# Strassen's algorithm for the down projection of ten channel groups, laid between the blocks of the up projection

## The chip, the cores and the metric

The kernel runs on one core of one Trainium2 chip. The metric is the device time of one execution in microseconds; a profiled execution gives the trace, whose span goes from the first to the last instruction. The core has five engines that matter here: TensorE (PE in the trace, PEld for its weight loads), VectorE (DVE), ScalarE (ACT), GpSimd (POOL) and SyncE (SP), which issues the transfers.

## What is computed

One layer of a bidirectional encoder, 512 tokens by 2048 channels, all in float32: a norm, one input projection, windowed attention beside chunked spatial gating, an output projection, and then the gated MLP, which is where the change is.

```python
def conv_ffn(h, w_up, conv_w, conv_b, w_down):
    a = h @ w_up                              # (512, 2048) x (2048, 11264)
    a = depthwise_conv(a, conv_w) + conv_b    # width 3 over the positions
    g, u = a[..., :D_FF], a[..., D_FF:]       # D_FF = 5632
    return (silu(g) * u) @ w_down             # (512, 5632) x (5632, 2048)
...
x = x + conv_ffn(rmsnorm(x, norm2_g), w_up, conv_w, conv_b, w_down)
return rmsnorm(x, final_g)
```

## The kernel before

Every large product is made of three matmuls in the type float32r. Each operand is split into a high part (a cast on ACT) and a low part (the operand minus its high part, on DVE), and `mm3` (L77 to L80) adds high x high, high x low and low x high in one PSUM bank. Weights come in units of 128 x 1024 floats (512 KB): `weights` (L65 to L75) loads a unit on SP's queue (L72), casts it on ACT (L73) and subtracts on DVE (L74). The pool `wp` has three buffers each for the unit as loaded, its high part and its low part.

The MLP has 44 tiles of 128 channels, in 11 groups of four (`NGRP`, `GF`). `up(i)` (L432 to L457) makes tile i: four units with 24 matmuls of 512 tokens each, for two PSUM banks (gate and linear part). In the last unit the first bank gets its 12 matmuls before the second. Then the tile is drained: for each bank the product with the norm (`a`, L445, DVE), the middle tap of the convolution (`c`, L448, ACT) and the two outer taps (L450 and L451, DVE), and then the SiLU (L454, ACT), the product (`sg`, L455, DVE), and the split of the result into `ah` and `al` (L456 ACT, L457 DVE).

`down(g, act)` (L466) takes a group of four tiles as 512 channels of the inner dimension: for each of four blocks of 512 output columns two units of `w_down`, and for each of four token tiles one PSUM bank with 4 x 3 matmuls (`down_part`, L459), added to the residual stream `x2[t][c]` on DVE (L464). The loop over the groups writes the four `up` blocks of group g and behind them `down(g - 1)`. The last group's down projection (from L486) runs token tile by token tile with the final norm behind each; its weights are split in `split` (L82).

PSUM has eight banks: four in the pool `psm` (the up blocks take two at a time) and four in `pss` (the down projection and all small products). SBUF has 64 slots of 128 x 512 floats in `big` (`slot`): sixteen hold `x2`, 32 the split input `hs` of the MLP. The pool `oct` has four tiles of 8 KB a partition, in the MLP for `ah` and `al`. The order in which an engine gets its instructions is drawn up when the program is built; it follows the text, but an instruction that is ready can go ahead of one that is not.

Of the kernel before, what the change touches and what calls it, by code (L numbers as in the profile page):

```python
# [47 lines left out]
def hymba_block(ctx, tc, xT, x, w_in, w_up, w_out, w_down, wsT, cols, brow, frow, srow, rel, out):  # L48
    nc = tc.nc
    const = ctx.enter_context(tc.tile_pool(name="const", bufs=1))  # L50
    big = ctx.enter_context(tc.tile_pool(name="big", bufs=NSLOT))
    wp = ctx.enter_context(tc.tile_pool(name="wp", bufs=3))
    oct = ctx.enter_context(tc.tile_pool(name="oct", bufs=4))
    tmp = ctx.enter_context(tc.tile_pool(name="tmp", bufs=2))
    small = ctx.enter_context(tc.tile_pool(name="small", bufs=4))
    psm = ctx.enter_context(tc.tile_pool(name="psm", bufs=4, space=bass.MemoryType.PSUM))
    pss = ctx.enter_context(tc.tile_pool(name="pss", bufs=4, space=bass.MemoryType.PSUM))

    def f(ap):
        return ap.bitcast(F32)  # L60
# [3 lines left out]

    def weights(src, name, parts=1):  # L65
        st = wp.tile([P, 1024], F32, tag="wst", name=f"st_{name}")
        hi = wp.tile([P, 1024], F32R, tag="whi", name=f"hi_{name}")
        lo = wp.tile([P, 1024], F32R, tag="wlo", name=f"lo_{name}")
        n = 1024 // parts
        for i in range(parts):  # L70
            cs = slice(i * n, (i + 1) * n)
            nc.sync.dma_start(st[:, cs], src[:, cs])  # L72
            nc.scalar.copy(hi[:, cs], st[:, cs])  # L73
            nc.vector.tensor_tensor(lo[:, cs], st[:, cs], f(hi[:, cs]), op=ALU.subtract)  # L74
        return hi, lo  # L75

    def mm3(ps, a, b, start, stop):  # L77
        nc.tensor.matmul(ps, a[0], b[0], start=start, stop=False)  # L78
        nc.tensor.matmul(ps, a[0], b[1], start=False, stop=False)  # L79
        nc.tensor.matmul(ps, a[1], b[0], start=False, stop=stop)  # L80

# [11 lines left out]
    def rsqrt_v(v, n, name, pool=None):  # L93
        """1 / sqrt(v) over [P, n], by Newton's iteration; -RS_K / sqrt(v) if n is 1."""
        pool = pool or small
        r = pool.tile([P, n], F32, tag=f"{name}_r" if pool is const else f"rs_r{n}", name=f"{name}_r")
        t = small.tile([P, n], F32, tag=f"rs_t{n}", name=f"{name}_t")
        nc.vector.tensor_single_scalar(t.bitcast(I32), v.bitcast(I32), 1, op=ALU.logical_shift_right)
        nc.vector.tensor_scalar(r.bitcast(I32), t.bitcast(I32), -1.0, float(0x5F3759DF), op0=ALU.mult, op1=ALU.add)
        for i in range(3):  # L100
            if n == 1:
                nc.vector.scalar_tensor_tensor(t, r, v, r, op0=ALU.mult, op1=ALU.mult)
                nc.vector.scalar_tensor_tensor(r, t, RS_C[i], r, op0=ALU.add, op1=ALU.mult)
            else:
# [12 lines left out]
    col = const.tile([P, N_COLS], F32, name="col")  # L117
# [119 lines left out]
    for t in range(NT):  # L237
# [192 lines left out]

    # ---- gated MLP with the convolution over positions
    def up(i, ah, al):  # L432
        pst = [psm.tile([P, S], F32, tag="m", name=f"up{i}_{j}") for j in range(2)]
        for u in range(4):
            hi, lo = weights(w_up[4 * i + u], f"u{i}_{u}")
            hv = hi.rearrange("p (k j c) -> p k j c", k=4, c=P)
# [6 lines left out]
        for j in range(2):  # L443
# [8 lines left out]
            cv.append(t)  # L452
        sg = slot(F32, f"sg{i}")
        nc.scalar.activation(sg, cv[0], AF.Silu)  # L454
        nc.vector.tensor_tensor(sg, sg, cv[1], op=ALU.mult)  # L455
        nc.scalar.copy(ah, sg)  # L456
        nc.vector.tensor_tensor(al, sg, f(ah), op=ALU.subtract)  # L457

    def down_part(g, act, c, t, un, cs=slice(0, S)):  # L459
        ps = pss.tile([P, S], F32, tag="s", name=f"dn{g}{c}{t}")[:, cs]  # L460
        for k in range(GF):
            a = tuple(z[:, k, t * P : (t + 1) * P] for z in act)
            mm3(ps, a, tuple(z[:, cs] for z in un[k]), k == 0, k == GF - 1)
        nc.vector.tensor_tensor(x2[t][c][:, cs], x2[t][c][:, cs], ps, op=ALU.add)  # L464

    def down(g, act):  # L466
        for c in range(4):
            un = []
            for u in range(2):
                hi, lo = weights(w_down[(g * 4 + c) * 2 + u], f"d{g}{c}{u}")  # L470
                un += [(hi[:, :S], lo[:, :S]), (hi[:, S:], lo[:, S:])]
            for t in range(NT):
                down_part(g, act, c, t, un)

    acts = {}
    for g in range(NGRP):
        ah = oct.tile([P, GF, S], F32R, tag="oct", name=f"ah{g}")
        al = oct.tile([P, GF, S], F32R, tag="oct", name=f"al{g}")
        for k in range(GF):
            up(GF * g + k, ah[:, k, :], al[:, k, :])  # L480
        acts[g] = (ah, al)
        if g >= 1:
            down(g - 1, acts.pop(g - 1))

    # ---- the last group of channels, token tile by token tile, and the final norm
    g = NGRP - 1  # L486
    fg = [slot(F32, f"fg{c}") for c in range(4)]
    un = []
    for c in range(4):
        un.append([])  # L490
        for u in range(2):
            st = wp.tile([P, 1024], F32, tag="wst", name=f"st_l{c}{u}")
            nc.sync.dma_start(st, w_down[(g * 4 + c) * 2 + u])
            for k in range(2):
                un[c].append(split(st[:, k * S : (k + 1) * S], f"dl{c}{u}{k}"))
        nc.sync.dma_start(fg[c], frow[c * S : (c + 1) * S].partition_broadcast(P))
        nc.vector.tensor_scalar_mul(fg[c], fg[c], -1.0 / RS_K)
    for t in range(NT):
        ssf = small.tile([P, 5], F32, tag="ssf", name=f"ssf{t}")
        pre = small.tile([P, 1], F32, tag="pre", name=f"pre{t}")  # L500
        for c in range(4):
            xt = x2[t][c]
            if c < 3:
                down_part(g, acts[g], c, t, un[c])
                junk = slot(F32, f"jf_{c}{t}")
                nc.scalar.activation(junk, xt, AF.Square, accum_out=ssf[:, c : c + 1])
                nc.vector.tensor_tensor(xt, xt, fg[c], op=ALU.mult)
            else:
                junk = slot(F32, f"jf_{c}{t}")
                for i in range(2):  # L510
                    cs = slice(i * 256, i * 256 + 256)
                    down_part(g, acts[g], c, t, un[c], cs)
                    nc.scalar.activation(junk[:, cs], xt[:, cs], AF.Square, accum_out=ssf[:, c + i : c + i + 1])
# [17 lines left out]
def _units(w, ncols):  # L531
    """[K, n] -> [units, 128, 1024]: for each ncols columns, 1024 / ncols row tiles a unit."""
    K, n = w.shape
# [9 lines left out]
def _layout(x, norm1_g, w_in, gmlp_v_norm_g, gmlp_ws, gmlp_b, attn_sink, attn_out_norm_g,  # L543
# [10 lines left out]
    w3 = np.concatenate([_units(wo[:1024], 512), _units(wo[1024:], 512)])  # L554
    w4 = np.concatenate([_units(wd[g * GF * P : (g + 1) * GF * P], 512) for g in range(NGRP)])
    cw, cb = np.asarray(conv_w)[0], np.asarray(conv_b)[0]
# [34 lines left out]
```

## Time and profile before

| | us |
|---|---|
| median of 3 runs | 2002.8 |
| lowest and highest run | 1999.89 and 4076.22 |
| span of the profiled execution | 1999.4 |
| PE busy in that span | 1986.3 |
| DVE busy | 993.2 |
| ACT busy | 623.0 |
| matmuls (records) | 9016 |

The table's busy times are sums over the whole span. PE's matmuls are pipelined: a row's duration is longer than the time to the next row. A view by windows tells how busy each engine was in a stretch and at what share of its full speed TensorE's clock was granted; a timeline gives each instruction's start and duration, and in brackets how long its engine had been idle and who released it.

### The profile page before, as it was taken

What the parts mean: (1) busy time and instruction counts of PE and PEld (TensorE: products, weight loads), DVE (VectorE), ACT (ScalarE), POOL (GpSimd) and SP (SyncE); (2) the same over time, 40 slices, a digit from 0 to 9 for tenths busy, and PEclk for the clock granted to TensorE, in tenths of its full rate; (3) what the DMA queues carried; (4) which work ended last, traced back from release to release, by engine and by line L of the source; (5) the groups of instructions that cost most, each with busy time, mean ns of one, the idle gap of its engine ahead of it and who ended that gap; (6) DMA issues with size and microseconds to landing.
All of it is one profiled execution on the core that took longest, in us unless ns stands there. A gap on an engine that the chain in (4) does not pass through costs nothing.

```text
span 1999.4 us, 21966 instructions
## 1 busy us (share of the span) xinstructions
PE 1986.3 (99%) x9016; PEld 1648.8 (82%) x9016; DVE 993.2 (50%) x1350; ACT 623.0 (31%) x825; POOL 56.2 (3%) x60
## 2 busy tenths in 40 slices
PE   9999999999999999999999999999999999999998
PEld 7988888888888888888888888888888888888887
DVE  7376573434454454444445444444445454454466
ACT  6243442312333332323323223232232232322333
POOL 5001101000000000000000000000000000000000
PEclk9999999999999999999999999999999999999999
DMA  6222232532223323233232232222332223322242
GB/s 219 86 73 74 74 106 94 170 100 88 95 85 100 101 84 106 96 95 102 88 106 95 95 102 99 95 95 95 98 102 95 95 95 98 103 94 96 95 148 84
DMA packets 59572, 201.06 MB, mean 101 GB/s; under 512 B 6864, under 2 KB 7120, under 8 KB 59472
## 3 DMA queue, kind: packets, MB, share of 16 engines
q1 hardware_dynamic: 59472, 199.67, 30.5%
q8 instruction: 70, 1.15, 0.2%
q14 instruction: 30, 0.25, 0.0%
HBM read 195.44 MB, written 4.19 MB: 100 GB/s over the span
## 4 chain that ended last, share of the span: by engine, by line
PE 97%; issue 1%; DVE 1%; POOL 0%; ACT 0%; DMA 0%; SPq 0%; ACTq 0%; DVEq 0%; POOLq 0%
PE up L80 16%; PE up L78 16%; PE up L79 16%; PE dn L79 8%; PE dn L78 8%; PE dn L80 8%; PE pj L78 3%; PE pj L79 3%; PE pj L80 3%; PE u L78 1%; PE u L79 1%; PE u L80 1%; PE vg_ps L78 1%; PE vg_ps L79 1%; PE vg_ps L80 1%; PE g L79 1%
## 5 line engine op out<-in xcount | busy, mean ns | idle before, releaser
L80 PE MATMUL up<-h_h,lo_u 128*128 128x512 f32 x1408 | 547.9, 389 | 0.0
L78 PE MATMUL up<-h_h,hi_u 128*128 128x512 f32 x1408 | 547.9, 389 | 0.0
L79 PE MATMUL up<-h_l,hi_u 128*128 128x512 f32 x1408 | 547.8, 389 | 0.0
L74 DVE TENSOR_TENSOR lo_u<-st_u,hi_u 128x1024 fp32r<-128x1024 f32 x176 | 215.3, 1224 | 362.8 <-ACT hi_u L73 362.8
L73 ACT CAST hi_u<-st_u 128x1024 fp32r<-128x1024 f32 x176 | 185.6, 1055 | 471.5 <-PE up L79 377.8
L79 PEld LDWEIGHTS up<-h_l,hi_u 128*128 128x128 f32 x1408 | 264.4, 188 | 54.8
L80 PEld LDWEIGHTS up<-h_h,lo_u 128*128 128x128 f32 x1408 | 264.4, 188 | 54.8
L78 PEld LDWEIGHTS up<-h_h,hi_u 128*128 128x128 f32 x1408 | 264.4, 188 | 54.6
L78 PE MATMUL dn<-hi_d,ah 128*128 128x512 f32 x640 | 249.0, 389 | 0.0
L79 PE MATMUL dn<-lo_d,ah 128*128 128x512 f32 x640 | 249.0, 389 | 0.0
L80 PE MATMUL dn<-hi_d,al 128*128 128x512 f32 x640 | 249.0, 389 | 0.0
L464 DVE TENSOR_TENSOR x<-x,dn 128x512 f32<-128x512 f32 (+1 forms) x180 | 121.2, 674 | 138.2 <-PE dn L80 137.2
L73 ACT CAST hi_d<-st_d 128x1024 fp32r<-128x1024 f32 x80 | 84.4, 1055 | 306.3 <-PE dn L80 208.2
L74 DVE TENSOR_TENSOR lo_d<-st_d,hi_d 128x1024 fp32r<-128x1024 f32 x80 | 97.8, 1223 | 137.1 <-ACT hi_d L73 137.1
L78 PEld LDWEIGHTS dn<-hi_d,ah 128*128 128x128 f32 x640 | 120.2, 188 | 25.0
L79 PEld LDWEIGHTS dn<-lo_d,ah 128*128 128x128 f32 x640 | 120.2, 188 | 24.9
L80 PEld LDWEIGHTS dn<-hi_d,al 128*128 128x128 f32 x640 | 120.2, 188 | 24.9
L74 DVE TENSOR_TENSOR lo_i<-st_i,hi_i 128x1024 fp32r<-128x1024 f32 (+1 forms) x57 | 72.8, 1277 | 75.6 <-ACT hi_i L73 75.4
L448 ACT ACTIVATE c<-a,col 128x512 f32<-128x512 f32 x88 | 71.8, 816 | 120.8 <-DVE a L445 120.8
L73 ACT CAST hi_i<-st_i 128x1024 fp32r<-128x1024 f32 (+1 forms) x57 | 58.8, 1033 | 121.9 <-PE u L79 38.7
L74 DVE TENSOR_TENSOR lo_o<-st_o,hi_o 128x1024 fp32r<-128x1024 f32 x32 | 39.2, 1225 | 95.5 <-ACT hi_o L73 95.5
L450 DVE SCALAR_TENSOR_TENSOR c<-a,col,c 128x511 f32<-128x511 f32 x88 | 65.8, 748 | 38.9 <-ACT c L448 38.9
(243 smaller groups left out, 2264.3 us busy)
## 6 DMA issues: line engine op xcount, KB each, us to landing
st_u<-in_w_up SPq DMA_DIRECT2D x176, 512.0 KB, 3.3
st_d<-in_w_down SPq DMA_DIRECT2D x80, 512.0 KB, 3.3
st_i<-in_w_in SPq DMA_DIRECT2D x55, 512.0 KB, 3.3
st_o<-in_w_out SPq DMA_DIRECT2D x32, 512.0 KB, 3.3
xg<-in_xT SPq DMA_DIRECT2D x16, 256.0 KB, 4.8
x<-in_x SPq DMA_DIRECT2D x16, 256.0 KB, 5.7
st_l<-in_w_down SPq DMA_DIRECT2D x8, 512.0 KB, 3.5
out<-x SPq DMA_DIRECT2D x16, 256.0 KB, 2.9
```

The lines of the kernel that those rows point to most:

```text
L73: nc.scalar.copy(hi[:, cs], st[:, cs])
L74: nc.vector.tensor_tensor(lo[:, cs], st[:, cs], f(hi[:, cs]), op=ALU.subtract)
L78: nc.tensor.matmul(ps, a[0], b[0], start=start, stop=False)
L79: nc.tensor.matmul(ps, a[0], b[1], start=False, stop=False)
L80: nc.tensor.matmul(ps, a[1], b[0], start=False, stop=stop)
L448: nc.scalar.activation(t, a, AF.Identity, scale=w[1], bias=col[:, C_CB + j * 44 + i : C_CB + j * 44 + i + 1])
L450: nc.vector.scalar_tensor_tensor(t[:, 1:], a[:, : S - 1], w[0], t[:, 1:], op0=ALU.mult, op1=ALU.add)
L464: nc.vector.tensor_tensor(x2[t][c][:, cs], x2[t][c][:, cs], ps, op=ALU.add)
```

## The change

The groups 0 to 9 no longer use `down`. Their 512 tokens, 512 channels and 2048 columns are cut into halves (tokens: 256 and 256; channels: the even and the odd of the four tiles; columns: for each m in 0 and 1 the blocks m and 2 + m), and for each m the eight products of quarters are replaced by seven after Strassen, in the form with shared sums. `act_forms` makes the seven left factors (three plain quarters' splits beside four sums' splits: 11, 12, 22, s1, s2, s3, s4) once a group, from a float32 tile `act`. `down` makes the right factors from four loaded quarters (three plain ones, t1, t2, t3, t4), some in place, splits them with `halves`, and adds the products to the residual tiles and to `accu`, which collects what three of the four output quarters share over all groups. A product is twelve matmuls of 512 columns on two banks; two of the seven go on in banks that were read before.

A group's part is written as four functions, `first` and `second` for m = 0 and m = 1, and each is called behind one of the next group's four `up` blocks: `first` (four products: 11, s3, 12, 22) behind the first and third, `second` (s1, s2, s4) behind the second and fourth. `up` no longer splits its result. After the loop `accu` is added to the residual tiles and the last group's activations are split; its down projection is as before.

The pools `wp` and `oct` are closed ahead of the MLP. New pools stand in their place: `wq` with three buffers each for high and low parts, `raw` with six for loaded units and for t3, `acp` with one for `act`, `afp` with seven for the left factors. The layout of `w_down` in memory is changed to fit the quarters; a load is still 512 KB.

```diff
+    front.close()
+    wp = ctx.enter_context(tc.tile_pool(name="wq", bufs=3))
+    raw = ctx.enter_context(tc.tile_pool(name="raw", bufs=6))
+    acp = ctx.enter_context(tc.tile_pool(name="acp", bufs=1))
+    afp = ctx.enter_context(tc.tile_pool(name="afp", bufs=7))
...
-        sg = slot(F32, f"sg{i}")
-        nc.scalar.activation(sg, cv[0], AF.Silu)
-        nc.vector.tensor_tensor(sg, sg, cv[1], op=ALU.mult)
-        nc.scalar.copy(ah, sg)
-        nc.vector.tensor_tensor(al, sg, f(ah), op=ALU.subtract)
+        nc.scalar.activation(cv[0], cv[0], AF.Silu)
+        nc.vector.tensor_tensor(dst, cv[0], cv[1], op=ALU.mult)
...
+    def act_forms(g, act):
+        q = {(th, kh): act[:, kh::2, th * 256 : (th + 1) * 256] for th in range(2) for kh in range(2)}
...
+        put("11", q[0, 0])
+        put("s3", sum2(q[0, 0], q[1, 0], ALU.subtract, "s3"))
+        put("12", q[0, 1])
+        put("22", q[1, 1])
+        s1 = sum2(q[1, 0], q[1, 1], ALU.add, "s1")
+        put("s1", s1)
+        s2 = sum2(s1, q[0, 0], ALU.subtract, "s2")
+        put("s2", s2)
+        put("s4", sum2(q[0, 1], s2, ALU.subtract, "s4"))
+        return out
...
+        def product(a, st, name, pst, start):
+            hi, lo = halves(st, f"{name}{n}")
+            for t in range(2):
+                for k in range(2):
+                    w = tuple(z[:, k * S : (k + 1) * S] for z in (hi, lo))
+                    mm3(pst[t], tuple(z[:, k, t * P : (t + 1) * P] for z in af[a]), w, start and k == 0, k == 1, True)
...
+        def into(dst, pst):
+            for d, ps in zip(dst, pst):
+                nc.vector.tensor_tensor(d, d, ps, op=ALU.add)
...
+        def first():
+            b["11"] = q(0, 0)
+            b["12"], b["22"] = q(0, 1), q(1, 1)
+            pa = bank("dp1")
+            product("11", b["11"], "b11", pa, True)
+            into(accu[m], pa)
+            t3 = raw.tile([P, 1024], F32, tag="raw", name=f"t3_{n}")
+            sub(t3, b["22"], b["12"])
+            pb = bank("dp7")
+            product("s3", t3, "t3", pb, True)
+            into(c22, pb)
+            b["21"] = q(1, 0)
+            product("12", b["21"], "b21", pa, False)
+            into(c11, pa)
+            b["t1"] = sub(b["12"], b["12"], b["11"])
+            b["t2"] = sub(b["11"], b["22"], b["t1"])
+            t4 = sub(b["21"], b["21"], b["t2"])
+            product("22", t4, "t4", pb, False)
+            into(c21, pb)
+
+        def second():
+            pa = bank("dp5")
+            product("s1", b["t1"], "t1", pa, True)
+            into(c22, pa)
+            pb = bank("dp6")
+            product("s2", b["t2"], "t2", pb, True)
+            into(accu[m], pb)
+            product("s4", b["22"], "b22", pa, False)
+            into(c12, pa)
...
     for g in range(NGRP):
+        act = acp.tile([P, GF, S], F32, tag="act", name=f"act{g}")
+        parts = [p for m in range(2) for p in down(g - 1, m, af)] if g else [None] * GF
         for k in range(GF):
-            up(GF * g + k, ah[:, k, :], al[:, k, :])
-        acts[g] = (ah, al)
-        if g >= 1:
-            down(g - 1, acts.pop(g - 1))
+            up(GF * g + k, act[:, k, :])
+            if parts[k]:
+                parts[k]()
+        if g < NGRP - 1:
+            af = act_forms(g, act)
+    for m in range(2):
+        for t in range(2):
+            for d in (x2[t][2 + m], x2[2 + t][m], x2[2 + t][2 + m]):
+                nc.vector.tensor_tensor(d, d, accu[m][t], op=ALU.add)
```

## Rows read from the trace of the kernel before

**Rows 1.** The page: the span, and each engine's busy us, share, instructions.
```profile
span 1999.4 us, 21966 instructions
...
PE 1986.3 (99%) x9016; PEld 1648.8 (82%) x9016; DVE 993.2 (50%) x1350; ACT 623.0 (31%) x825; POOL 56.2 (3%) x60
```

**Rows 2.** Waits of PE: who for whom, total, times, longest.
```profile
PE r_ps L144 <- POOL xsq L166: 2.0, 1, 2.0
```

**Rows 3.** Windows: stretch, length, busy PE, PEld, DVE, ACT, POOL, clock, DMA, GB/s.
```profile
50.00:200.00 150.00, 149.87 (x792) 126.61 (x791) 84.00 (x155) 51.77 (x102) 10.00 (x20) 1.00 0.24 78
...
1180.00:1304.00 124.00, 124.00 (x549) 102.71 (x548) 60.14 (x71) 34.36 (x39) 0.00 (x0) 1.00 0.30 98
...
1990.00:1999.40 9.40, 0.26 (x3) 0.06 (x1) 3.46 (x14) 1.84 (x4) 0.00 (x0) 0.69 0.32 112
```

**Rows 4.** Timeline around the end of an up block: start, duration, engine, instruction.
```profile
1245.23 1.23 DVE L74 TENSOR_TENSOR lo_d<-st_d,hi_d 128x1024 fp32r<-128x1024 f32 x1 [4.26 <-ACT hi_d L73]
...
1249.57 0.39 PE L78 MATMUL dn<-hi_d,ah 128*128 128x512 f32 x1
...
1250.08 0.68 DVE L445 TENSOR_TENSOR a<-up,r_b 128x512 f32<-128x512 f32 x1
...
1250.68 1.22 DVE L74 TENSOR_TENSOR lo_d<-st_d,hi_d 128x1024 fp32r<-128x1024 f32 x1
...
1251.82 0.75 DVE L450 SCALAR_TENSOR_TENSOR c<-a,col,c 128x511 f32<-128x511 f32 x1
...
1252.49 0.69 DVE L464 TENSOR_TENSOR x<-x,dn 128x512 f32<-128x512 f32 x1
...
1253.10 0.75 DVE L451 SCALAR_TENSOR_TENSOR c<-a,col,c 128x511 f32<-128x511 f32 x1
...
1253.95 0.69 DVE L455 TENSOR_TENSOR sg<-sg,c 128x512 f32<-128x512 f32 x1
...
1254.67 0.62 ACT L456 CAST ah<-sg 128x512 fp32r<-128x512 f32 x1 [2.53 <-DVE sg L455]
...
1256.83 0.39 PE L80 MATMUL dn<-hi_d,al 128*128 128x512 f32 x1
```

**Rows 5.** The page's groups (count, busy us, mean ns) and its loads.
```profile
L78 PE MATMUL dn<-hi_d,ah 128*128 128x512 f32 x640 | 249.0, 389 | 0.0
...
L73 ACT CAST hi_d<-st_d 128x1024 fp32r<-128x1024 f32 x80 | 84.4, 1055 | 306.3 <-PE dn L80 208.2
...
st_d<-in_w_down SPq DMA_DIRECT2D x80, 512.0 KB, 3.3
```

**Rows 6.** Timeline of DVE where ready work stands back to back.
```profile
1260.38 1.23 DVE L74 TENSOR_TENSOR lo_d<-st_d,hi_d 128x1024 fp32r<-128x1024 f32 x1 [1.76 <-ACT hi_d L73]
1261.52 0.68 DVE L464 TENSOR_TENSOR x<-x,dn 128x512 f32<-128x512 f32 x1
1262.12 1.22 DVE L74 TENSOR_TENSOR lo_d<-st_d,hi_d 128x1024 fp32r<-128x1024 f32 x1
```

**Rows 7.** Timeline of DVE and PE where the MLP begins.
```profile
545.76 1.23 DVE L74 TENSOR_TENSOR lo_u<-st_u,hi_u 128x1024 fp32r<-128x1024 f32 x1 [4.17 <-ACT hi_u L73]
...
549.69 0.39 PE L80 MATMUL pj<-hi_o,gm7s_l 128*128 128x512 f32 x1
...
551.77 0.47 PE L78 MATMUL up<-h_h,hi_u 128*128 128x512 f32 x1
```

**Rows 8.** Timeline of PE after its longest wait.
```profile
42.49 1.05 PE L144 MATMUL r_ps<-ones,xsq 128*128 128x1 f32 x8 [1.95 <-POOL xsq L166]
...
44.76 0.63 PE L80 MATMUL g<-x_h,lo_i 128*128 128x512 f32 x1
...
47.74 0.49 PE L78 MATMUL g<-x_h,hi_i 128*128 128x512 f32 x1
```

**Rows 9.** Windows early in the span, columns as in rows 3.
```profile
10.00:14.00 4.00, 3.20 (x15) 2.30 (x13) 2.36 (x3) 3.81 (x6) 2.58 (x2) 1.00 1.04 408
42.00:46.00 4.00, 3.50 (x16) 2.98 (x17) 3.73 (x9) 0.50 (x1) 0.44 (x1) 0.82 0.36 118
```

More of the change, by code (lines that the diff above doesn't have):

```diff
@@ L51, in hymba_block @@
     big = ctx.enter_context(tc.tile_pool(name="big", bufs=NSLOT))
-    wp = ctx.enter_context(tc.tile_pool(name="wp", bufs=3))
-    oct = ctx.enter_context(tc.tile_pool(name="oct", bufs=4))
     tmp = ctx.enter_context(tc.tile_pool(name="tmp", bufs=2))
     small = ctx.enter_context(tc.tile_pool(name="small", bufs=4))
+    front = ctx.enter_context(ExitStack())
+    pools = {"wp": front.enter_context(tc.tile_pool(name="wp", bufs=3))}
+    oct = front.enter_context(tc.tile_pool(name="oct", bufs=4))
     psm = ctx.enter_context(tc.tile_pool(name="psm", bufs=4, space=bass.MemoryType.PSUM))
@@ L65, in weights @@
     def weights(src, name, parts=1):
+        wp = pools["wp"]
         st = wp.tile([P, 1024], F32, tag="wst", name=f"st_{name}")
@@ L75, in weights, with mm3 @@
         return hi, lo
[L77 to L80, printed above, removed]
+    def mm3(ps, a, b, start, stop, free=False):
+        nc.tensor.matmul(ps, a[0], b[0], start=start, stop=False, skip_group_check=free)
+        nc.tensor.matmul(ps, a[0], b[1], start=False, stop=False, skip_group_check=free)
+        nc.tensor.matmul(ps, a[1], b[0], start=False, stop=stop, skip_group_check=free)
     def split(src, name, scale=None):
@@ L429, in hymba_block, with halves, load, up @@
     rb2 = bcast_rows(r2, "r2", const, "rb1")
-    def up(i, ah, al):
+    front.close()
+    wp = ctx.enter_context(tc.tile_pool(name="wq", bufs=3))
+    pools["wp"] = wp
+    raw = ctx.enter_context(tc.tile_pool(name="raw", bufs=6))
+    acp = ctx.enter_context(tc.tile_pool(name="acp", bufs=1))
+    afp = ctx.enter_context(tc.tile_pool(name="afp", bufs=7))
+    def halves(st, name):
+        hi = wp.tile([P, 1024], F32R, tag="whi", name=f"hi_{name}")
+        lo = wp.tile([P, 1024], F32R, tag="wlo", name=f"lo_{name}")
+        nc.scalar.copy(hi, st)
+        nc.vector.tensor_tensor(lo, st, f(hi), op=ALU.subtract)
+        return hi, lo
+    def load(src, name):
+        st = raw.tile([P, 1024], F32, tag="raw", name=f"st_{name}")
+        nc.sync.dma_start(st, src)
+        return st
+    def up(i, dst):
         pst = [psm.tile([P, S], F32, tag="m", name=f"up{i}_{j}") for j in range(2)]
         for u in range(4):
-            hi, lo = weights(w_up[4 * i + u], f"u{i}_{u}")
+            hi, lo = halves(load(w_up[4 * i + u], f"u{i}_{u}"), f"u{i}_{u}")
             hv = hi.rearrange("p (k j c) -> p k j c", k=4, c=P)
@@ L452, in up @@
             cv.append(t)
-        sg = slot(F32, f"sg{i}")
-        nc.scalar.activation(sg, cv[0], AF.Silu)
-        nc.vector.tensor_tensor(sg, sg, cv[1], op=ALU.mult)
-        nc.scalar.copy(ah, sg)
-        nc.vector.tensor_tensor(al, sg, f(ah), op=ALU.subtract)
+        nc.scalar.activation(cv[0], cv[0], AF.Silu)
+        nc.vector.tensor_tensor(dst, cv[0], cv[1], op=ALU.mult)
+    accu = [[slot(F32, f"accu{m}{t}") for t in range(2)] for m in range(2)]
+    for row in accu:
+        for a in row:
+            nc.gpsimd.memset(a, 0.0)
@@ new lines, in act_forms, with sum2, put @@
+    def act_forms(g, act):
+        q = {(th, kh): act[:, kh::2, th * 256 : (th + 1) * 256] for th in range(2) for kh in range(2)}
+        def sum2(a, b, op, name):
+            t = slot(F32, f"{name}_{g}")
+            v = t.rearrange("p (k c) -> p k c", k=2)
+            nc.vector.tensor_tensor(v, a, b, op=op)
+            return v
+        out = {}
+        def put(name, v):
+            t = afp.tile([P, 1024], F32R, tag="af", name=f"af{name}_{g}")
+            hi = t[:, :S].rearrange("p (k c) -> p k c", k=2)
+            lo = t[:, S:].rearrange("p (k c) -> p k c", k=2)
+            nc.scalar.copy(hi, v)
+            nc.vector.tensor_tensor(lo, v, f(hi), op=ALU.subtract)
+            out[name] = (hi, lo)
+        put("11", q[0, 0])
[8 more added lines that the diff above has]
+        return out
@@ new lines, in down, with q, sub, bank @@
+    def down(g, m, af):
+        n = f"{g}{m}"
+        b = {}
+        def q(kh, nh):
+            return load(w_down[((g * 2 + m) * 2 + kh) * 2 + nh], f"d{n}{kh}{nh}")
+        def sub(out, x, y):
+            nc.vector.tensor_tensor(out, x, y, op=ALU.subtract)
+            return out
+        def product(a, st, name, pst, start):
[4 more added lines that the diff above has]
+                    mm3(pst[t], tuple(z[:, k, t * P : (t + 1) * P] for z in af[a]), w, start and k == 0, k == 1, True)
+        def bank(name):
+            return [pss.tile([P, S], F32, tag="s", name=f"{name}{n}{t}") for t in range(2)]
+        def into(dst, pst):
+            for d, ps in zip(dst, pst):
+                nc.vector.tensor_tensor(d, d, ps, op=ALU.add)
+        c11, c12, c21, c22 = ([x2[2 * th + t][2 * nh + m] for t in range(2)] for th in range(2) for nh in range(2))
+        def first():
[26 more added lines that the diff above has]
+            into(c12, pa)
+        return first, second
@@ L461, in down_part @@
         for k in range(GF):
-            a = tuple(z[:, k, t * P : (t + 1) * P] for z in act)
+            a = tuple(z[k][:, t * P : (t + 1) * P] for z in act)
             mm3(ps, a, tuple(z[:, cs] for z in un[k]), k == 0, k == GF - 1)
         nc.vector.tensor_tensor(x2[t][c][:, cs], x2[t][c][:, cs], ps, op=ALU.add)
[L466 to L475, printed above, removed]
+    af = None
     for g in range(NGRP):
-        ah = oct.tile([P, GF, S], F32R, tag="oct", name=f"ah{g}")
-        al = oct.tile([P, GF, S], F32R, tag="oct", name=f"al{g}")
+        act = acp.tile([P, GF, S], F32, tag="act", name=f"act{g}")
+        parts = [p for m in range(2) for p in down(g - 1, m, af)] if g else [None] * GF
         for k in range(GF):
-            up(GF * g + k, ah[:, k, :], al[:, k, :])
-        acts[g] = (ah, al)
-        if g >= 1:
-            down(g - 1, acts.pop(g - 1))
-    g = NGRP - 1
+            up(GF * g + k, act[:, k, :])
[7 more added lines that the diff above has]
+                nc.vector.tensor_tensor(d, d, accu[m][t], op=ALU.add)
+    g = NGRP - 1
+    acts = []
+    for z in range(2):
+        acts.append([slot(F32R, f"al{z}_{k}") for k in range(GF)])
+    for k in range(GF):
+        nc.scalar.copy(acts[0][k], act[:, k, :])
+        nc.vector.tensor_tensor(acts[1][k], act[:, k, :], f(acts[0][k]), op=ALU.subtract)
     fg = [slot(F32, f"fg{c}") for c in range(4)]
@@ L491, in hymba_block @@
         for u in range(2):
-            st = wp.tile([P, 1024], F32, tag="wst", name=f"st_l{c}{u}")
-            nc.sync.dma_start(st, w_down[(g * 4 + c) * 2 + u])
+            st = load(w_down[(g * 4 + c) * 2 + u], f"l{c}{u}")
             for k in range(2):
@@ L503, in hymba_block @@
             if c < 3:
-                down_part(g, acts[g], c, t, un[c])
+                down_part(g, acts, c, t, un[c])
                 junk = slot(F32, f"jf_{c}{t}")
@@ L511, in hymba_block @@
                     cs = slice(i * 256, i * 256 + 256)
-                    down_part(g, acts[g], c, t, un[c], cs)
+                    down_part(g, acts, c, t, un[c], cs)
                     nc.scalar.activation(junk[:, cs], xt[:, cs], AF.Square, accum_out=ssf[:, c + i : c + i + 1])
@@ L554, in _layout @@
     w3 = np.concatenate([_units(wo[:1024], 512), _units(wo[1024:], 512)])
-    w4 = np.concatenate([_units(wd[g * GF * P : (g + 1) * GF * P], 512) for g in range(NGRP)])
+    w4 = wd[: (NGRP - 1) * GF * P].reshape(NGRP - 1, 2, 2, P, 2, 2, 512).transpose(0, 5, 2, 4, 3, 1, 6)
+    w4 = np.concatenate([w4.reshape(-1, P, 1024), _units(wd[(NGRP - 1) * GF * P :], 512)])
     cw, cb = np.asarray(conv_w)[0], np.asarray(conv_b)[0]
@@ L578 @@
     from concourse.bass_utils import run_bass_kernel_spmd
-    nc = bacc.Bacc("TRN2", target_bir_lowering=False, num_devices=1)
+    nc = bacc.Bacc("TRN2", target_bir_lowering=False, num_devices=1, dynamic_dma_scratch_size=1024)
     arrays, args = {}, []
```

## The prediction

> **What bounds the kernel now.** I read the page's busy times first [rows 1]: TensorE (PE) is busy 1986.3 of 1999.4 us, VectorE (DVE) half of it. A pipelined PE that looks busy need not be dense, so next the waits of PE [rows 2]: the longest of three is 2.0 us, once in the whole span. Then the windows [rows 3]: 124.00 of 124 us in a stretch of the gated MLP, and 149.87 of 150 even in the attention, where DVE has 84 us of tangled work. So PE's own issue is the bound, and the unit of account is its pitch, not the 389 ns that a row shows for one matmul. The rows at 1249.57 and 1256.83 [rows 4] are 32 matmuls apart: 7.26 / 32 = 0.2268 us. A matmul taken away is worth that, as long as PE stays dense. The question is only whether it does.
>
> **The change, part by part.**
>
> *Matmuls removed.* Before, a group's down projection is 4 column tiles x 4 token tiles x 4 channel tiles x 3 = 192 matmuls (640 x 3 / 10 in the page's groups [rows 5]). Now it is 2 halves m x 7 products x 2 token tiles x 2 channel tiles x 3 = 168, all again with 512 columns, so I price them by the same pitch. 24 x 10 groups x 0.2268 = **54.4 us** less. Loads stay 8 of 512 KB a group.
>
> *DVE work added, a group.* The nearest rows are the subtraction of 128x1024 and the addition of 128x512 from a PSUM bank [rows 6]: in a row of ready work they start 1.14 us apart (1260.38 to 1261.52) and 0.60 apart (1261.52 to 1262.12). Added: 8 sums of weights and 6 more low parts (14 x 1.14 = 16.0), 12 more additions out of PSUM (28 instead of 16, 7.2), 4 sums and 3 more low parts of the activations (7 x 0.6 = 4.2): 27.4 us. DVE had 60.14 in 124 us [rows 3], 63.3 in a group's 576 x 0.2268 = 130.6; now 91 in 552 x 0.2268 = 125.2. ScalarE (ACT) gets six casts of 1.05 and three of 0.6 us more. On average both have room: neither is the bound. What can cost is a burst at one place.
>
> *Where the burst is.* Look at the end of an up block before [rows 4]. Call T the start of the first matmul after it (1249.57). DVE then does a, lo, stt, x+=dn, stt, mult at T+0.5, 1.1, 2.25, 2.9, 3.5 and 4.4. Two things are to be seen: the order is not the program text's (lo_d and the addition of dn slip in where the second stt is not ready), yet what stands earlier in the text goes first whenever it is ready. I carry this rule over. And lo_d at T+1.1 belongs to the third weight unit: with 3 buffers for high and low parts, the unit whose buffer comes free at T is split only then. Before, each buffer held 24 matmuls (5.44 us) of work; a Strassen product uses one for 12 (2.72 us), so the stock in front of PE halves.
>
> For `first()`, times after T, DVE at 0.61 a 512-wide and 1.14 a 1024-wide operation: a 0.5, low part of b21 1.1 (its buffer came free at T), stt 2.25, accu+= 2.9, stt 3.5, accu+= 4.2, mult 4.8, c22+= 5.4 and 6.0, t4 6.6, c11+= 7.8 and 8.4, low part of t4 9.0 to 10.2. PE does product 11 to 2.7, s3 to 5.4 (t3 and its parts are made in the idle 4 us between the lo_u before T), 12 to 8.2, and then wants "22", whose weights are ready at 10.2. What else is ready is the next up block: its unit got a buffer at 2.7 and ACT cast it, but its low part stands behind all of the above. High parts alone allow 4 matmuls (two in each of two banks), 0.9 us, to 9.1. The stall: 10.2 - 9.1 = **1.15 us**, twice a group, 20 times: **23 us**. Between the ends: nothing, if the order drawn up slips the next unit's low part in earlier, and 3.2 us (8.2 to 11.3, that part behind t4's) if no matmul can use the high parts alone. I take the middle value because the DVE list has no hole in it.
>
> For `second()` the three products last 8.2 us. Without more work DVE comes to the next unit's low part at 6.6 to 7.8: no stall. After the fourth up block (nine times with both) `act_forms` stands in between: low parts of forms 12 and 22, and s1, 3 x 0.61 and two c12+= push that part to 9.7 to 10.8, against PE's 9.1: 1.8 us, 9 times: **16 us** (ends: 0, and 5 if all eight remaining form operations go ahead of it). Forms 11 and s3 need only channel tiles 0 and 2 and come a block earlier.
>
> *Moves and waits.* SP's queue now has `raw` with 6 buffers; between `first` and `second` three of them hold t1, t2, b22. The remaining three feed the up block as the three st buffers did, at 3.3 us to landing [rows 5] against 5.44 us of PE work a unit: hidden, and if a load were late it would cost at most its 3.3 us.
>
> *The new pools.* They stand on the memory of wp and oct. Before, the first up block's second unit had its low part at 545.76, ahead of the last projection's end [rows 7]. If the new buffers wait for the old ones' last reader (549.69), then load 3.3, cast 1.05, subtraction 1.23 give 549.9 + 5.6 = 555.5, against 551.77: **3.7 us**, once (0, if only overlapping buffers wait). Nothing covers it but the 16 transposes, which that sum holds.
>
> *The end.* The last group's fourth activation is now covered by `second` (8.2 us) and not by 43.5 us of down projection. Its low part stands behind 12 additions of accu, of which six can go early: 6.6 + 8 x 0.61 + 0.6, about 12 us after T. PE has meanwhile channel tiles 0 to 2 of four output tiles, 36 x 0.2268 = 8.2 us more, to 16.4: nothing; without that cover 4 us. The chain after the last matmul, in the window from 1990 to 1999.4 [rows 3], stays.
>
> *The clock.* After PE's wait to 42.49 seven matmuls take from 44.76 to 47.74 [rows 8], 0.426 us each, where 7 x 0.2268 = 1.59 would do: 1.4 us lost. The granted clock of 42 to 46 us is 0.82 [rows 9]: for a while it was at its lower level, 1.2 of 2.4 GHz. After the 0.8 us that are missing in 10 to 14 us it stayed 1.00 [rows 9]. So I charge **1.4 us** for the 3.7 us gap, and none for the 29 short ones. The Trainium skill ("TensorE: Matmul & The Clock Gate", section "A second HAM failure mode: psum-queue depth-cycling") says that frequent short idle moments between groups of matmuls are enough to throw the clock to and fro. The trace agrees for one gap of 2.1 us and not for 0.8. That is a rival below.
>
> **Sum.** 1999.4 - 54.4 + 23 + 16 + 3.7 + 1.4 = 1989 us of span. The three runs stand at 1999.89, 2002.8 and one far off; the two stand 0.5 and 3.4 above this span: **1990 us**, 0.6% below the median.
>
> **The rivals.**
>
> A, *the holes fill*: PE finds matmuls at every turn, as in the attention. Then 1999.4 - 54.4 + 5.1 = 1950, some 1952 us as a run. For it: 149.87 of 150 us [rows 3] with DVE bursts as tangled. Against it: there each buffer held 5.44 us of PE work, here 2.72, and the 10 us of DVE work after T are ordered ahead of what PE needs. To be faster by over 2% the 29 stalls must average below 0.4 us.
>
> C, *the stalls cool the clock* (slower): the place is the same 29 turns. If a turn costs 2.1 us of idling, as the gap before 42.49 (a wait of 1.95 and its start), and the clock then falls each time, it costs 2.1 + 1.4 = 3.5 us: 29 x 3.5 = 102, and 1999.4 - 54.4 + 102 + 5.1 = 2052, some 2054 us. From 1.7 us a turn the change loses, from 3.1 us it loses over 2%. Against it: I count 1.15 and 1.8, between 0.8 (no fall) and 2.1 (a fall). Where in between it tips no row shows. By the rule of the Trainium skill named above it would happen, at this time.
>
> DVE as the bound throughout (91 of 125 us) is ruled out, and fewer matmuls is plain counting.
>
> **How the numbers follow.** My forecast, stalls of about a microsecond or two that eat most of the gain, has 0.50; its own range is 1970 to 2012 (0.7 us a turn either way). A has 0.33, C 0.17. 2% is 40 us, about what a measurement here can tell from no change. Below 1962.7: A, 0.33. Above 2042.9: C, 0.17. Between: 0.50. For 8 in 10 the range takes nearly all of A and the lower part of C: 1950 to 2040.
>
> **What would show it.** Matmuls 9016 - 240 = 8776 (some records may be missing). PE's waits: 20 of about 1.2 us before t4's product, released by DVE (low part of t4 or of the next u unit), 9 of about 1.8 us after form operations, one of 3.7 us near 551.8. DVE total 993 + 10 x 27 = about 1270 us. PEclk full except after 551.8. PE without waits there means A; a clock below 1.00 in the groups means C. Waits on a DMA, or a pitch other than 0.227 in the new products, would mean I have missed the mechanism.

## The result and the profile after

The changed kernel takes 2076.43 us (median, 2075.67 to 2078.99) against 2001.95 of the kernel before in the same comparison: 1.0377 times as long, interval 1.0361 to 1.0392. One of the four runs of the kernel before took 4076.22 us; it counts in the median and not in the ratio. The forecast was 1990 us with 1950 to 2040. The change is slower by 75 us, where a small gain was expected.

The page of the changed kernel, which answers to [rows 1] (span; busy us, share and instructions of each engine):

```profile
span 2075.1 us, 21993 instructions
...
PE 1997.6 (96%) x8776; PEld 1611.8 (78%) x8776; DVE 1263.0 (61%) x1692; ACT 690.2 (33%) x915; POOL 58.1 (3%) x64
```

The counts are as predicted: 8776 matmuls, 240 fewer, and DVE at 1263 us (about 1270 foretold). But PE is busy for 11 us *longer* with 240 matmuls less, and 64 us more of the span are not busy. So two things happened: matmuls follow one another more slowly, and PE waits. The waits of PE after, which answer to [rows 2] (who waits for whom: total us, times, longest):

```profile
PE up L82 <- DVE lo_u L446: 36.6, 9, 4.1
PE dp L80 <- ACT hi_t L445: 14.1, 20, 1.0
PE up L80 <- ACT hi_u L445: 6.8, 21, 2.5
PE dn L81 <- DVE dl_l L89: 6.3, 2, 6.0
```

Nine long waits, twenty short ones before the fourth product of `first` (each with a second, shorter one behind it), one at the boundary and one at the tail: the places are those that the prediction named, but for the last. To get a sum I took the start of every matmul in both traces and put each distance from one start to the next, less the 0.2268 us of before, into one of these rows (a distance counts as pitch below 0.3 us, as clock where it lies in a stretch at the lower clock, else as a gap; how the distances at the edge of a stretch are sorted moves about 1 us between the rows on the clock and on the gaps):

| us of span | before | after | difference |
|---|---|---|---|
| 240 matmuls fewer, at 0.2268 | | | -54.4 |
| slower pitch | 1.8 | 37.3 | +35.5 |
| lower clock | 1.5 | 16.5 | +15.0 |
| gaps ahead of `up` matmuls (the 9 long ones, the turns, the boundary) | 0.3 | 53.1 | +52.8 |
| gaps ahead of `dp` matmuls (t4's product, the 20 turns) | 0 | 19.6 | +19.6 |
| gaps ahead of `dn` matmuls (tail) | 0 | 7.7 | +7.7 |
| gaps before the MLP, and rest | 10.6 | 10.4 | -0.2 |
| sum | | | +76.0 (spans: +75.7) |

**The slower pitch.** It is in the same timeline as the fast one. PE of the kernel after: the first and last of 24 `dp` matmuls, the first and last of 16 `up` matmuls:

```profile
1224.07 0.39 PE L80 MATMUL dp<-hi_t,afs 128*128 128x512 f32 x1
...
1229.28 0.39 PE L82 MATMUL dp<-hi_b,af 128*128 128x512 f32 x1
...
1234.47 0.40 PE L82 MATMUL up<-h_h,lo_u 128*128 128x512 f32 x1
...
1237.96 0.39 PE L82 MATMUL up<-h_h,lo_u 128*128 128x512 f32 x1
```

5.21 / 23 = 0.2265 us for the new products, 3.49 / 15 = 0.2327 for the unchanged up projection, with PE full and the clock at 1.00. The slow pitch is not only in the MLP: in the input projection, where the diff touches nothing, 512-column matmuls start 232 to 233 ns apart too. Common to the slow ones is that one operand lies in the 64 slots and the other in a pool behind them; the new products have both operands in pools behind them.

**The nine long waits.** DVE and PE of the kernel after around the fourth block's end (T = 1184.97, the first matmul behind it, 36 matmuls before 1193.13):

```profile
1189.82 0.68 DVE L476 TENSOR_TENSOR act<-c,c 128x512 f32<-128x512 f32 x1
1190.42 1.27 DVE L541 TENSOR_TENSOR accu<-accu,dp 128x512 f32<-128x512 f32 x2
1191.62 0.68 DVE L493 TENSOR_TENSOR s<-act 128x512 f32<-128x512 f32 x1
1192.22 0.68 DVE L541 TENSOR_TENSOR x<-x,dp 128x512 f32<-128x512 f32 x1
1192.82 0.68 DVE L493 TENSOR_TENSOR s<-act 128x512 f32<-128x512 f32 x1
1193.42 0.68 DVE L541 TENSOR_TENSOR x<-x,dp 128x512 f32<-128x512 f32 x1
1194.02 0.68 DVE L503 TENSOR_TENSOR afs<-s,afs 128x512 fp32r<-128x512 f32 x1
1194.62 1.28 DVE L503 TENSOR_TENSOR af<-act,af 128x512 fp32r<-128x512 f32 x2
1195.82 0.68 DVE L503 TENSOR_TENSOR afs<-s,afs 128x512 fp32r<-128x512 f32 x1
1196.42 0.68 DVE L493 TENSOR_TENSOR s<-s,act 128x512 f32<-128x512 f32 x1
1197.03 1.22 DVE L446 TENSOR_TENSOR lo_u<-st_u,hi_u 128x1024 fp32r<-128x1024 f32 x1
...
1193.13 0.40 PE L80 MATMUL up<-h_h,hi_u 128*128 128x512 f32 x1
...
1198.30 0.50 PE L82 MATMUL up<-h_h,lo_u 128*128 128x512 f32 x1 [4.07 <-DVE lo_u L446]
```

PE does what the prediction said to the tenth: from T + 8.2 four matmuls with the high parts alone, to T + 9.1. But seven form operations and two additions stand ahead of the next unit's low part, which ends at T + 13.3. Then the clock. Windows of the kernel after (stretch, length, busy PE, PEld, DVE, ACT, POOL, clock, DMA, GB/s): around this wait, and around one of the short ones:

```profile
1196.00:1198.00 2.00, 0.00 (x0) 0.00 (x0) 2.00 (x3) 0.62 (x1) 0.00 (x0) 1.00 0.00 0
...
1200.00:1202.00 2.00, 2.00 (x6) 1.51 (x6) 2.00 (x3) 0.10 (x1) 0.00 (x0) 0.50 0.44 174
...
1230.00:1232.00 2.00, 1.11 (x4) 0.63 (x5) 2.00 (x4) 2.00 (x3) 0.00 (x0) 1.00 0.00 0
1232.00:1234.00 2.00, 2.00 (x10) 1.65 (x9) 2.00 (x2) 0.53 (x1) 0.00 (x0) 1.00 0.56 160
```

After the 4.1 us wait the granted clock is 0.50, the lower of the two levels, and six matmuls start in 2 us; after the wait of 1.0 us and the 0.2 behind it the clock stays 1.00. It fell behind each of the nine long waits, at the boundary and at the tail, and behind none of the twenty turns.

**A turn of `first`.** DVE, ACT and PE of the kernel after, T = 1221.33:

```profile
1228.28 1.22 DVE L526 TENSOR_TENSOR st_d<-st_d,st_d 128x1024 f32<-128x1024 f32 x1
...
1230.66 1.23 DVE L446 TENSOR_TENSOR lo_t<-st_d,hi_t 128x1024 fp32r<-128x1024 f32 x1
1231.80 2.35 DVE L446 TENSOR_TENSOR lo_u<-st_u,hi_u 128x1024 fp32r<-128x1024 f32 x2
...
1229.58 1.05 ACT L445 CAST hi_t<-st_d 128x1024 fp32r<-128x1024 f32 x1 [5.66 <-DVE st_d L526]
1230.53 2.00 ACT L445 CAST hi_u<-st_u 128x1024 fp32r<-128x1024 f32 x2
...
1230.68 0.73 PE L80 MATMUL dp<-hi_t,af 128*128 128x512 f32 x2 [1.01 <-ACT hi_t L445]
1231.63 0.50 PE L80 MATMUL up<-h_h,hi_u 128*128 128x512 f32 x1 [0.21 <-ACT hi_u L445]
```

t4 is made at T + 7.0 (6.6 foretold) and its low part is ready at T + 10.6 (10.2 foretold). Both halves of the next up unit come behind it on both engines.

**The tail.** DVE and PE of the kernel after:

```profile
2013.35 2.49 DVE L597 TENSOR_TENSOR x<-x,accu 128x512 f32<-128x512 f32 x4
2015.76 2.49 DVE L606 TENSOR_TENSOR al<-act,al 128x512 fp32r<-128x512 f32 x4
2018.16 3.69 DVE L89 TENSOR_TENSOR dl_l<-st_l,dl_h 128x512 fp32r<-128x512 f32 x6
...
2012.47 0.39 PE L80 MATMUL dn<-dl_h,al 128*128 128x512 f32 x1
2018.90 0.80 PE L81 MATMUL dn<-dl_l,al 128*128 128x512 f32 x1 [6.04 <-DVE dl_l L89]
```

The low parts of the last down projection's *weights* stand behind the additions of accu and the four low parts of the activations. PE gets one matmul done, then waits 6.0 us.

### The profile page after: what moved, and what is told of

Same layout as the page of the kernel before. It is cut to its first block, busy times and chain, and to the rows that moved or that the text cites. A ratio compares the mean times of both kernels' runs of the same rounds, so it can differ in the third digit from the quotient of the medians.

```text
span 2075.1 us, 21993 instructions
## 1 busy us (share of the span) xinstructions
PE 1997.6 (96%) x8776; PEld 1611.8 (78%) x8776; DVE 1263.0 (61%) x1692; ACT 690.2 (33%) x915; POOL 58.1 (3%) x64
## 4 chain that ended last, share of the span: by engine, by line
PE 87%; DVE 8%; ACT 2%; issue 1%; DMA 1%; POOL 0%; SPq 0%; ACTq 0%; DVEq 0%; POOLq 0%
PE up L82 16%; PE up L80 16%; PE up L81 15%; PE dp L82 5%; PE dp L81 5%; PE dp L80 4%; PE pj L80 3%; PE pj L82 3%; PE pj L81 3%; PE u L80 1%; PE vg_ps L82 1%; PE vg_ps L81 1%; PE vg_ps L80 1%; PE u L82 1%; PE u L81 1%
## 5 line engine op out<-in xcount | busy, mean ns | idle before, releaser
L82 PE MATMUL up<-h_h,lo_u 128*128 128x512 f32 x1408 | 563.1, 401 | 36.6 <-DVE lo_u L446 36.6
L80 PE MATMUL up<-h_h,hi_u 128*128 128x512 f32 x1408 | 564.3, 401 | 6.8 <-ACT hi_u L445 6.8
L446 DVE TENSOR_TENSOR lo_t<-st_d,hi_t 128x1024 fp32r<-128x1024 f32 x60 | 73.5, 1225 | 175.0 <-ACT hi_t L445 175.0
L445 ACT CAST hi_t<-st_d 128x1024 fp32r<-128x1024 f32 x60 | 63.0, 1050 | 259.1 <-PE up L81 182.0
L541 DVE TENSOR_TENSOR x<-x,dp 128x512 f32<-128x512 f32 x200 | 130.7, 680 | 0.0
L446 DVE TENSOR_TENSOR lo_b<-st_d,hi_b 128x1024 fp32r<-128x1024 f32 x60 | 73.5, 1225 | 81.0 <-ACT hi_b L445 81.0
L445 ACT CAST hi_b<-st_d 128x1024 fp32r<-128x1024 f32 x60 | 63.1, 1052 | 129.4 <-PE up L81 128.1
L81 PE MATMUL dp<-lo_t,afs 128*128 128x512 f32 x240 | 93.5, 390 | 0.0
L82 PE MATMUL dp<-hi_t,afs 128*128 128x512 f32 x240 | 93.4, 389 | 0.0
L80 PE MATMUL dp<-hi_t,afs 128*128 128x512 f32 x240 | 93.4, 389 | 0.0
L467 DVE TENSOR_TENSOR a<-up,r_b 128x512 f32<-128x512 f32 x88 | 60.5, 687 | 30.1 <-PE up L82 30.1
```

What stands on the lines that cost most here:

```text
L80: nc.tensor.matmul(ps, a[0], b[0], start=start, stop=False, skip_group_check=free)
L81: nc.tensor.matmul(ps, a[0], b[1], start=False, stop=False, skip_group_check=free)
L82: nc.tensor.matmul(ps, a[1], b[0], start=False, stop=stop, skip_group_check=free)
L445: nc.scalar.copy(hi, st)
L446: nc.vector.tensor_tensor(lo, st, f(hi), op=ALU.subtract)
L467: nc.vector.tensor_tensor(a, pst[j], rb2, op=ALU.mult)
```

## The experiments

The times of the kernel before in the comparisons below are 2001.2 to 2001.3 us. The first theory of the slower pitch (P in the expectations, where its rivals Q and R stand beside it) was that it goes by the distance of the two operands of a matmul in SBUF. As the programs lay out their memory, in the kernel before the slots begin at byte 23328 of a partition and the weights' pool 131072 bytes behind them; in the changed kernel the slots begin at 7968 and the weights' pool 134528 bytes behind them, since the small pools `tmp` and `small` (3456 bytes) were moved between them when `wp` and `oct` became pools that are closed early.

**e1, the slots' base alone.** The kernel before with

```diff
+ dynamic_dma_scratch_size=1024
```

in the program's constructor, which moves everything without changing the distances.

> The kernel before with one line of the change alone: the smaller scratch area for transfers (1024 bytes), which moves every SBUF tile down by 15360 bytes and leaves their distances as they were. In the changed kernel every matmul that reads a tile of the 64 slots starts about 232 ns after the one before it, also in the front part, whose code is the same, against 226.7 before; matmuls on other tiles keep 227. Theory P (the distance of the two operands' addresses sets the pitch): no change, 2000 us, pitch 226.7. Theory Q (the place in SBUF, or the scratch area itself, sets it): about 6700 matmuls x 5 ns = 33 us more, 2035 us. Theory R (another chip or another day): no change here nor in any kernel of this call.

Measured: 2001.04 us, ratio 0.9999 (0.9990 to 1.0009). Moving both operands by 15360 bytes (60 x 256) changes nothing.

**e2, the pools' order alone.** The kernel before with the changed kernel's order of pools and nothing else of the change:

```diff
+    tmp = ctx.enter_context(tc.tile_pool(name="tmp", bufs=2))
+    small = ctx.enter_context(tc.tile_pool(name="small", bufs=4))
     wp = ctx.enter_context(tc.tile_pool(name="wp", bufs=3))
     oct = ctx.enter_context(tc.tile_pool(name="oct", bufs=4))
-    tmp = ctx.enter_context(tc.tile_pool(name="tmp", bufs=2))
-    small = ctx.enter_context(tc.tile_pool(name="small", bufs=4))
```

> The kernel before with another line of the change alone: the small pools tmp and small stand ahead of the weights' pool in SBUF, which moves the weights (and the tiles of oct) by 3456 bytes against the slots; 3456 is 13.5 x 256. Nothing else differs. Theory P (operands' distance): matmuls that take one operand from the weights and one from the slots go from 226.7 to about 232 ns, those of the down projection (weights and oct, which move together) stay; (9016 - 2160 - 384 and the small ones, some 6000) x 5 ns = 30 us more, about 2031 us. Theory Q (place or scratch area): no change, 2000 us. Theory R (chip): no change.

Measured: 2035.57 us, 1.0172 (1.0157 to 1.0187). P holds, Q and R fall: 34 us of the loss come from where 3456 bytes lie. The `dn` matmuls, whose operands both lie in the moved pools, kept 0.2268 us. That also speaks against a last rival, which e1 leaves open because its shift is a multiple of 256: that it is one operand's address alone that counts, and not the distance of the two.

**e8, e9, e10, how far apart.** The kernel before with one unused tile between slots and weights, of 256, 128 and 64 bytes a partition (in the diff 64, then 32 and 16 floats):

```diff
+    gap = ctx.enter_context(tc.tile_pool(name="gap", bufs=1))
+    nc.vector.memset(gap.tile([P, 64], F32, name="gap_t")[:, :1], 0.0)
```

> The kernel before with an unused tile of 256 bytes behind the slots, so that the weights stand 131072 + 256 bytes behind them; nothing else differs. The slow kernels had a distance of 128 more than a multiple of 256 (134528), the fast ones a multiple of 2048. If the distance counts in steps of 256: pitch 226.7 and 2000 us. If it counts in steps of 512 or more: pitch some 232 in the up blocks and some 2030 us.

> The kernel before with one unused tile of 128 bytes a partition between the 64 slots and the weights' pools; nothing else differs. Theory P (the pitch of a matmul rises when its two operands' addresses differ by 128 bytes beyond a multiple of 256, which is what 3456 bytes of small pools make of it in the changed kernel): the up blocks' matmuls start 232 to 233 ns apart and those of the down projection (both operands in the moved pools) stay at 227; about 2034 us. Rival P2 (it is the 3456 bytes as such, or which pools come first, and not the remainder): pitch 226.7 everywhere, 2001 us.

> The same with 64 bytes. Theory P in its narrow form (only an odd multiple of 128 costs): 226.7 ns, 2001 us. In a wide form (anything but a multiple of 256 costs): 232 to 233 ns, about 2034 us; or something between, if the cost grows with the remainder.

Measured, single runs: 2002.8, 2035.77 and 2034.77 us (the runs of the kernel before lie within 3 us of one another in these comparisons). The same window in e8, e9 and e10, where [rows 3] has 549 matmuls (columns as above):

```profile
1180.00:1304.00 124.00, 124.00 (x549) 102.68 (x548) 60.20 (x71) 35.37 (x39) 0.00 (x0) 1.00 0.30 95
```
```profile
1180.00:1304.00 124.00, 124.00 (x538) 100.56 (x537) 57.49 (x67) 35.71 (x40) 0.00 (x0) 1.00 0.28 94
```
```profile
1180.00:1304.00 124.00, 124.00 (x538) 100.26 (x537) 58.22 (x68) 35.49 (x40) 0.00 (x0) 1.00 0.29 94
```

PE is full and its clock 1.00 in all three, and 549, 538 and 538 matmuls start. So 128 and 64 bytes cost the same 34 us, 256 costs nothing: fast were the distances that are multiples of 256 bytes (131072, 131328), slow those that are not (134528, 131200, 131136). Remainders other than 64 and 128 weren't tried, and no run shows what in the chip does it.

**e3, the distance mended in the changed kernel.** The tile `gap` with 160 floats, which makes the distance 135168 = 528 x 256.

> The changed kernel with an unused tile of 640 bytes behind the slots, which moves the weights' buffers so that they stand to the slots as in the kernel before (a multiple of 512 bytes apart). No instruction of the computation changes. Theory P: pitch of the up blocks back to 226.7, some 36 us less, about 2040 us; waits of PE as they were (9 of 4.1 us at the forms, 20 of about 1 us before t4's product). Theory Q or R: no change, 2076 us.

Measured: 2050.10 us, 1.0247 (1.0232 to 1.0262), 26.3 less than after, not 36. By the sum of starts the pitch did give back 34.4 us of span, but the lower clock cost some 6.5 more and the gaps about 1: after four of the nine long waits, instead of one, the clock now stayed low twice as long (6.8 us and not 3.4). Why it did is not shown; e5, without the long waits, gets that part back.

**e4, the forms alone.** `act_forms` is called in the middle of the next up block, behind its second unit, instead of at the end of the group:

```diff
-    def up(i, dst):
+    def up(i, dst, mid=None):
...
+            if u == 2 and mid:
+                mid()
...
-            up(GF * g + k, act[:, k, :])
+            up(GF * g + k, act[:, k, :], mid if k == 0 else None)
...
-            af = act_forms(g, act)
+            af = {}
+            mid = lambda g=g, act=act, af=af: act_forms(g, act, af)
```

> The changed kernel with the left factors of the next group made in the middle of the following up block (behind its second unit) in the text instead of ahead of that block. Nothing is left out. Theory: the 11 operations of the forms stand ahead of the next unit's low part on VectorE, which costs PE 4.35 us nine times and lets the clock fall for 3.4 us each time (1.5 us lost): 9 x 5.85 = 53 us less, about 2023 us, clock 1.00 in the groups. Rival: the burst only moves; the next unit's low part is then late by the same work elsewhere: within 15 us of 2076.

Measured: 2024.00 us, 1.0116 (1.0101 to 1.0131), 52.4 less than after. The waits of PE in e4:

```profile
PE dp L80 <- ACT hi_t L445: 14.0, 20, 0.7
PE up L80 <- ACT hi_u L445: 6.8, 21, 2.5
PE dn L81 <- DVE dl_l L89: 6.0, 1, 6.0
...
PE up L82 <- DVE lo_u L446: 0.2, 1, 0.2
```

The nine waits of 4.1 us are one of 0.2. By the starts 39.8 us of gaps went and some 11 us of lower clock. The twenty turns are still there, and between the boundary and the tail no stretch at the lower clock is left: the short gaps don't cause one.

**e5, both.**

> The changed kernel with both edits: the unused tile of 640 bytes (distance of weights and slots as before) and the left factors made in the middle of the following up block. If the two costs are independent: 2024.0 - 34 (the pitch rows of the run with the tile alone) = 1990 us, which is 0.6% below the kernel before (same within 2%). If the idle time given back by one is taken by the other, as a fifth of it was in the run with the tile alone: up to 1998.

Measured: 1991.31 us, 0.9951 (0.9937 to 0.9966). Together -85.1, where -26.3 and -52.4 make -78.7: the difference of 6.4 is, within the sum's error, the some 6.5 us that the lower clock cost e3 at the long waits.

**e6, the turns of `first`.** On top of e5 the next up block's first unit gets its halves right behind product 12, ahead of the work for t4 (`i` is the number of the next up block, and `unit` loads and splits one of its units):

```diff
             product("12", b["21"], "b21", pa, False)
+            pre[i, 0] = unit(i, 0)
             into(c11, pa)
...
-            hi, lo = halves(load(w_up[4 * i + u], f"u{i}_{u}"), f"u{i}_{u}")
+            hi, lo = pre.pop((i, u), None) or unit(i, u)
```

> The same with a third edit: the high and low part of the next up block's first unit stand in the text of first() right behind product 12, ahead of the additions of c11 and of t4. Theory: PE's 20 gaps before and behind t4's product (1.08 and 0.61 us, some 1.45 us a turn with the slow restarts) come from the next unit's low part standing behind t4's on VectorE. They go: 20 x 1.45 = 29 us less than the run with two edits, about 1961 us, more than 2% below the kernel before. Rival: t4's product then comes too late for something else (its PSUM banks, c21), and the gap moves behind it: no gain, within 10 us of the run with two edits.

Measured: 1961.65 us, 0.9803 (0.9788 to 0.9818), 29.7 less than e5. Whether that is the expected "more than 2% below the kernel before" the interval (0.9788 to 0.9818) leaves open. What is left in the waits of PE in e6, beside those of the first 50 us:

```profile
PE dn L83 <- DVE dl_l L91: 6.1, 1, 6.1
PE up L82 <- ACT hi_u L447: 2.6, 1, 2.6
```

One wait at the tail and one at the boundary. The order alone was at fault: not one operation less, and PE has matmuls while t4 is made.

**e7, the tail.** On top of e6 the twelve additions of accu are written elsewhere: six behind the last group's third part, six behind the split of the second block of weights.

```diff
+    def flush(m):
+        for t in range(2):
+            for d in (x2[t][2 + m], x2[2 + t][m], x2[2 + t][2 + m]):
+                nc.vector.tensor_tensor(d, d, accu[m][t], op=ALU.add)
...
+            if g == NGRP - 1 and k == 2:
+                flush(0)
...
+        if c == 1:
+            flush(1)
```

> The same with a fourth edit, at the end: the 12 additions of accu no longer stand ahead of the last group's splits; six stand behind the last group's third part, six behind the second block's weights. PE's one wait of 6.0 us for dl_l, and the fall of the clock behind it (1.5 us), should go: 7.5 us less than the run with three edits, about 1953 us. Rival: dl_l is late for want of free slots or of VectorE, whatever the order: no change.

Measured: 1959.28 us, 0.9792 (0.9776 to 0.9809): 2.4 less than e6 by the medians and 0.6 by the spans of the profiled executions, not the 7.5 expected; the runs of the two overlap (e6 from 1960.14, e7 up to 1960.61). PE's waits for the low parts in e7, and DVE around the longest:

```profile
PE dn L83 <- DVE dl_l L91: 4.1, 3, 3.7
...
1898.47 0.68 DVE L594 TENSOR_TENSOR x<-x,accu 128x512 f32<-128x512 f32 x1
1899.07 0.68 DVE L617 TENSOR_TENSOR al<-act,al 128x512 fp32r<-128x512 f32 x1
1899.67 0.68 DVE L594 TENSOR_TENSOR x<-x,accu 128x512 f32<-128x512 f32 x1
1900.28 0.68 DVE L91 TENSOR_TENSOR dl_l<-st_l,dl_h 128x512 fp32r<-128x512 f32 x1
1900.88 0.68 DVE L594 TENSOR_TENSOR x<-x,accu 128x512 f32<-128x512 f32 x1
1901.48 0.68 DVE L91 TENSOR_TENSOR dl_l<-st_l,dl_h 128x512 fp32r<-128x512 f32 x1
```

The additions that are ready slip in between the halves that PE waits for, although they are written behind them; the longest wait only went from 6.1 to 3.7 us. The first low part comes earlier, but the ones behind it now start 1.20 us apart (1900.28, 1901.48), where the six of the kernel after stand back to back in 3.69 us, and PE waits twice more. That it is the weights' split itself that comes too late, behind the activations', is a reading of these rows and not shown; an earlier split wasn't tried.

## Why the prediction failed, point by point

The foretold span was 1989 us and the profiled one is 2075.1. Of the 86 us between them 35.5 are the pitch (point 1), 23 the size of the nine gaps (point 3), 14 the clock behind them (point 4), some 8 the tail and 7 the turns of `first`, less 1 at the boundary. So two steps failed by weight: a pitch that was taken as given for all matmuls, and the sum of DVE work ahead of the nine turns together with its clock.

1. *240 matmuls at the pitch of before, -54.4.* The count was right, and so is the price for the new products (0.2265). The step that failed is one that was never made: that every *other* matmul keeps its pitch when the pools are laid out anew. The diff shows `wp` and `oct` closed and new pools in their place, and the prediction followed that only for buffers and waits. It cost +35.5 us, 34 of them shown by e2 with nothing else of the change.
2. *`first`, 23 us.* The place, the times of t4 and DVE's order held; the size was 30 (by the gaps 19.6 ahead of `dp` and 10.7 of the `up` gaps that e4 leaves beyond the boundary; 29.7 by e6). One link was wrong: the next unit's high part was not cast early, as the step had it; on ACT too it stood behind t4's, so the four matmuls with high parts could not bridge the wait.
3. *The forms, 16 us.* The mechanism was right (e4), the size was not: nine gaps of 4.35 us are 39. Three form operations were counted ahead of the unit's low part, seven are in the rows: the sum for s3, its low part, that of s1 and the sum s2 besides. "Forms 11 and s3 come a block earlier" held for 11 alone. 4 x 0.60 = 2.4 us more than 1.8 is nearly the whole of it; the upper bound of 5 us held it. What kept s3 back, when DVE stood idle a block earlier, no row shows.
4. *The clock, 1.4 us once.* The price of a fall was right (16.5 us for 11 falls, 1.5 each); the number was wrong, since waits of 4.1 us were put down as 1.8. None for the short turns was right. The Trainium skill ("TensorE: Matmul & The Clock Gate", section "A second HAM failure mode: psum-queue depth-cycling"), which the prediction weighed, tells of a kernel in which frequent short idle moments between groups of matmuls set the clock going to and fro. The traces here don't show that: behind the twenty turns with waits of 1.0 and 0.2 us the clock stayed 1.00, and the gaps of 4.35 us behind which it fell come once in 133 us.
5. *The boundary, 3.7 us.* A wait of 2.5, with one fall of the clock behind it as foretold.
6. *The tail, nothing.* 7.7 us of gaps and a fall of the clock. The step looked at when the activations' low parts are ready and gave PE 36 matmuls meanwhile; those need the weights' low parts, which are on the same engine behind them.

Rival C, "the stalls cool the clock", had the right sign, but only in part the reason: the clock fell at 9 of the 29 turns, not at all of them, the nine gaps were twice as long as its 2.1 us, and it had no term for the pitch, nor had any other rival. That the measured time lies near its 2054 us is luck. Without the pitch the sum of what happened is 2076.4 - 35.5 = 2041 by the terms and 2050 by e3: slower still. And rival A, "the holes fill", is nearly what the same algorithm does when the order and the distance are mended: 1952 was its time, e6 and e7 reach 1961.65 and 1959.28.

## What to carry to other kernels

When a change opens or closes pools, work out where every unchanged operand comes to lie: here a shift of 64 or 128 bytes between the two operands of the matmuls cost 34 of 2000 us, more than half of what the algorithm saves, with PE at 100% and a full clock. When work is taken off a dense PE and given to another engine, list what that engine has ahead of the next weight halves at each turn, every operation with its count, since it is the order there and not the busy share that decides: the same operations take 2050 us in one order and 1962 in another. And price a gap with its restart, as here a gap of 4 us cost a fall of the clock too and one of 1 us didn't.

## What the hardware showed that was not expected

Matmuls of 512 columns of float32r start 226.7 ns apart when the two operands' addresses in a partition differ by a multiple of 256 bytes, and on average 232 to 234 ns when they differ by 64 or 128 more (e2, e9, e10), some 2.8% more. With 128 bytes the up projection's distances are of two kinds, near 229 and near 238 ns; with 64 bytes nearly all are 233 or 234, and there the `vg_ps` matmuls alone come with 229 to 230. 192 matmuls of 256 columns with the same operands' pools (`va`) took from 78.9 to 101.8 us in the kernel before and in the one after. The page's mean duration of a row shows it too, but as a smaller share: 395 ns against 389 for the `up` matmuls of e9 and e8, with `dn` at 389 in both. What it costs is read from the distance of the starts, or from the count in a window.
